# Moving a load, halving tile 0's modulation weights and reordering the first products of a decoder layer

## The chip, the cores and the metric

The kernel runs on one core of a Trainium2 chip. The metric is device time in microseconds (us) of one execution, a median over runs; lower is better. A core has TensorE (PE, matrix products into PSUM; its weight loads are PEld), VectorE (DVE), ScalarE (ACT) and GpSimd (POOL) for elementwise work, and SyncE (SP), which here only issues transfers. Each engine takes its instructions in program order and waits where one needs another engine's result or a transfer.

## The reference

One decoder layer on x (512 tokens by 1024 channels), conditioned by a vector c (1024), all in float32:

```python
cs = jax.nn.silu(c)
mod = cs @ w_ada[l] + b_ada[l]                       # 6 x 1024 numbers
shift1, scale1, gate1, shift2, scale2, gate2 = ...   # six pieces of mod
h = _rmsnorm(x, norm1_g[l]) * (1.0 + scale1) + shift1
proj = h @ w_in[l]                                   # queries, keys, values, gates
# sliding-window attention and differential attention on proj, gated merge, w_out,
# then a second modulated norm and a gated MLP with a causal convolution, final norm
```

The change concerns the first stage alone: shift1 and scale1, h, and the product of h with the first 768 columns of w_in.

## The kernel before, in words

The channels are cut into eight column tiles k = 0 to 7 of 128, the tokens into four row tiles. The first stage does, for every k: shift and scale of the tile's 128 channels (`mods[k]`), the normalised and modulated activations with channels on partitions (`hTh[k]`, 128 by 512), and their products with `w_in[128 k : 128 k + 128, 0:768]`, added into six PSUM banks `acc6` (six column groups, `FIRST` or `DONE` order). A float32 product is made of three passes on rounded operands: each operand is split into a high part (a cast, ScalarE) and a low part (the difference, VectorE), and the products high x high, low weight x high and high x low are added (`mm_k`: parts 0 and 2). `split_hi(k)` and `split_lo(k, part)` split the weights `w0[k]` into `w0h` and `w0l`; `h_tile(k)` writes `hTh[k]` and the unrounded `hf` on ScalarE, and `h_low(k)` their difference `hTl[k]` on VectorE. Tiles 6 and 7 of hT lie in a buffer called hThB, the others in hThA.

Shift and scale are sums over 1024 rows of w_ada. The weights of tile k (`adaw[k]`, 128 partitions by 2 by 8 by 128: j = 0 is scale, j = 1 shift, eight row groups kk) are multiplied by cs and added on VectorE and ScalarE (`ac_first`, `ac_ops`: `ac`), and a product with ones sums them over partitions (`reduce_mod`, into `pa`). For tile 0 TensorE multiplies five of the eight row groups directly with cs (`direct0`), VectorE adds up the other three (`add_a0`); for tile 1 TensorE does two of eight (`early_mod`, `direct`). `finish_mod(k)` makes `mods[k]` of `pa`, on VectorE and, for k > 0, one part on ScalarE. `h_turn(k)` (for tile 0, `turn`) transposes x on TensorE; x has been scaled by its reciprocal root mean square (`stat`, `root`, `scale_x`). `keep_warm` is TensorE filler whose result is not used.

What sets the order: in this stage SyncE issues all loads in one queue in the order of the code (`tc.manual_schedule` with SyncE): c, four tiles of x, then for each k the modulation weights and `w0[k]`, then small vectors, then the weights of later stages. TensorE, VectorE and ScalarE follow the code too. Work that the code writes further down, such as the casts of the next stage's weights (`split`, lines 127 to 129, the tiles `w_0_h` and so on, loaded in `load_cols`), is placed among the stage's instructions by a scheduler that works from estimated times, when the kernel is built.

## Time and profile before

| what | before |
|---|---|
| median of three runs | 685.49 us |
| lowest and highest run | 685.24, 686.26 us |
| span of the profiled execution, first to last instruction | 684.1 us |
| median of the runs less that span | 1.4 us |
| PE busy, and instructions | 675.3 us (99%), 4141 |
| DVE, ACT, POOL busy | 564.2, 384.5, 98.5 us |
| mean TensorE clock granted, of full speed | 0.998 |
| first product of the stage, last wait of PE | at 15.36 us, at 51.27 us |

The profiled execution's own time is its span, 684.1 us, and what lies around it before the first and after the last instruction; beside the median that is 1.4 us. In a row of the profile in order of time, the columns are the start in us from the first instruction, the duration in us, the engine, the line of the kernel, the operation, the tiles written and read, shapes and a count; in square brackets stands how long the engine had been idle and what ended that. SPq and ACTq are issues of transfers. In a row by stretches (A:B) the columns are the length, the busy time of PE, PEld, DVE, ACT and POOL with counts, then the granted clock of TensorE, the share of the transfer engines and GB/s; where only PE is shown, PE stands alone. In a row of waits: engine, tile and line that waited, for whom, total us, times, longest.

### The profile page before, as it was taken

Reading aid. Unit: us, or ns where it says so; the run is one execution under the profiler, and the core shown is the slowest. Engines: PE = TensorE matmul, PEld = TensorE weight load, DVE = VectorE, ACT = ScalarE, POOL = GpSimd, SP = SyncE. Lnnn points to the kernel's source line nnn. Section 1 sums busy time; section 2 is a strip of 40 time slices with the busy share of each in tenths; the row PEclk is TensorE's granted clock in tenths of the full one; section 3 lists DMA queues with packets and bytes.
Section 4 is the critical chain, followed back from the end, with each engine's and each line's share of the span. In section 5 each row is a group of like instructions: output and inputs, shape, how many; then the busy total and the mean of one; then the engine's idle time right before and its main releaser. Section 6 shows DMA issues by size and latency. Waiting matters only on the chain. (4 is left out here: it accounts for less than half of the span.)

```text
span 684.1 us, 11125 instructions
## 1 busy us (share of the span) xinstructions
PE 675.3 (99%) x4141; PEld 589.7 (86%) x4141; DVE 564.2 (82%) x1075; ACT 384.5 (56%) x688; POOL 98.5 (14%) x119
## 2 busy tenths in 40 slices
PE   9999999999999999999999999999999999999995
PEld 5887887878888888888899999999999998888885
DVE  4999875988796756974589988888888999979997
ACT  6776774546543223324377665666555665656765
POOL 3000000011012012021030111112120003440300
PEclk9999999999999999999999999999999999999999
DMA  9995422565456885659555788777978647995903
GB/s 304 349 296 181 144 62 64 163 166 162 144 157 181 255 246 158 217 144 345 187 93 109 170 216 212 180 165 207 216 194 216 153 170 186 191 205 146 166 1 123
DMA packets 117142, 123.89 MB, mean 181 GB/s; under 512 B 5063, under 2 KB 94184, under 8 KB 117088
## 3 DMA queue, kind: packets, MB, share of 16 engines
q1 hardware_dynamic: 97246, 95.11, 43.3%
q0 software_dynamic: 19648, 27.79, 24.1%
q8 instruction: 32, 0.52, 0.3%
q10 hardware_dynamic: 194, 0.28, 0.1%
q14 instruction: 22, 0.18, 0.1%
HBM read 118.97 MB, written 2.11 MB: 177 GB/s over the span
## 5 line engine op out<-in xcount | busy, mean ns | idle before, releaser
L1362 PE MATMUL up<-t,m_whi 128*128 128x256 f32 x512 | 93.1, 283 | 0.0
L1362 PEld LDWEIGHTS up<-t,m_whi 128*128 128x128 f32 x512 | 79.9, 192 | 0.0
L1362 PE MATMUL up<-t,m_wlo 128*128 128x256 f32 x256 | 72.4, 283 | 0.0
L1362 PE MATMUL up<-bh,p_whi 128*128 128x256 f32 x232 | 65.7, 283 | 0.0
L1362 PE MATMUL up<-bl,p_whi 128*128 128x256 f32 x232 | 65.7, 283 | 0.0
L1362 PE MATMUL up<-bh,p_wlo 128*128 128x256 f32 x232 | 65.7, 283 | 0.0
L952 POOL DMA_DIRECT2D arow<-arow x28 | 22.5, 804 | 247.8 <-DVE sd L821 123.6
L1362 PEld LDWEIGHTS up<-t,m_wlo 128*128 128x128 f32 x256 | 49.2, 192 | 0.0
L1271 POOL DMA_DIRECT2D s<-in_w_up_dram x21 | 26.9, 1353 | 141.3 <-DMA s<-in_w_up_dram 69.2
L1362 PEld LDWEIGHTS up<-bh,p_whi 128*128 128x128 f32 x232 | 44.5, 192 | 0.0
L1362 PEld LDWEIGHTS up<-bl,p_whi 128*128 128x128 f32 x232 | 44.5, 192 | 0.0
L1362 PEld LDWEIGHTS up<-bh,p_wlo 128*128 128x128 f32 x232 | 44.5, 192 | 0.0
L944 DVE SCALAR_TENSOR_TENSOR arow<-ra,cs,arow 128x512 f32<-128x512 f32 x56 | 41.8, 748 | 0.6
L1299 ACT CAST m_whi<-s 128x1024 fp32r<-128x1024 f32 x31 | 32.4, 1046 | 11.1 <-DVE s L1293 6.3
L1303 DVE TENSOR_TENSOR m_wlo<-s,m_whi 128x1024 fp32r<-128x1024 f32 x31 | 37.8, 1218 | 0.0
L1362 PE MATMUL up<-t,p_whi 128*128 128x256 f32 x176 | 32.2, 283 | 0.0
L1362 PEld LDWEIGHTS up<-t,p_whi 128*128 128x128 f32 x176 | 27.5, 192 | 0.0
L816 ACT ACTIVATE sd<-sd,dmx 128x128 f32<-128x128 f32 (+3 forms) x32 | 17.7, 557 | 17.3 <-DVE dmx L806 17.3
L1369 ACT ACTIVATE gT<-a,cv 128x512 f32<-128x512 f32 x22 | 17.7, 813 | 16.9 <-DVE a L1404 15.8
L1299 ACT CAST p_whi<-wa 128x1024 fp32r<-128x1024 f32 x18 | 18.7, 1041 | 12.6 <-PE up L1362 12.6
L1303 DVE TENSOR_TENSOR p_wlo<-wa,p_whi 128x1024 fp32r<-128x1024 f32 x18 | 22.0, 1222 | 3.8 <-ACT p_whi L1299 3.8
L1362 PE MATMUL up<-t,p_wlo 128*128 128x256 f32 x88 | 24.9, 283 | 0.0
(499 smaller groups left out, 2052.4 us busy)
## 6 DMA issues: line engine op xcount, KB each, us to landing
ra<-in_w_ada_dram SPq DMA_DIRECT2D x32, 512.0 KB, 4.9
wa<-in_w_up_dram SPq DMA_DIRECT2D x22, 512.0 KB, 4.2
s<-in_w_up_dram SPq DMA_DIRECT2D x21, 512.0 KB, 4.7
s<-in_w_up_dram POOLq DMA_DIRECT2D x21, 512.0 KB, 6.9
w<-in_w_in_dram SPq DMA_DIRECT2D x12, 512.0 KB, 5.0
a<-in_w_up_dram SPq DMA_DIRECT2D x11, 512.0 KB, 4.7
b<-in_w_down_dram SPq DMA_DIRECT2D x10, 512.0 KB, 4.2
adaw<-in_w_ada_dram SPq DMA_DIRECT2D x8, 512.0 KB, 6.3
```

Of the source, the lines that this page charges most:

```text
L816: exp = nc.scalar.activation(pm[m], pm[m], AF.Exp, bias=mx[:, m : m + 1], scale=slope, accum_out=ls)
L944: nc.vector.scalar_tensor_tensor(ac, r[:, a], cc, ac, ALU.mult, ALU.add)
L952: nc.gpsimd.dma_start(whole[0:n], whole[n : 2 * n], accum_op=ALU.add)
L1271: nc.gpsimd.dma_start(dst, upblock(*blk), accum_op=ALU.add)
L1299: nc.scalar.copy(W[J, name][0], R[J, SRC[name]])
L1303: nc.vector.tensor_sub(lo, R[J, SRC[name]], hi.bitcast(F32))
L1362: nc.tensor.matmul(o[u], w[:, k, cu], b[:, k], start=name in ("p1", "m5", "p2") and k == 0 and x == 0, stop=k == 3 and x == 2, skip_group_ ...
L1369: nc.scalar.activation(grow(j), av[J][:, u], AF.Identity, bias=cv[:, 66 + j : 67 + j], scale=cv[:, 44 + j : 45 + j])
```

## The change

- c is loaded from ScalarE's queue instead of SyncE's, where it was first.
- `adaw[0]` is loaded in four pieces instead of two: both halves of scale, then both of shift.
- VectorE no longer adds up any of tile 0's shift: TensorE multiplies all eight of its row groups, four before tile 3 of x is turned and four after.
- The filler of two products after tile 0's `finish_mod` is gone; `h_turn(1)` stands there.
- The first hT tile is written in two halves, one by VectorE and one by ScalarE.
- For k = 0 the products high x high of five groups come first, then those with the low weights.
- For tile 1 all direct products of scale and shift come early, the sixth group's products ahead of the sums, and `split_lo(1, 0)` after `finish_mod`.

```diff
@@ -163,7 +163,7 @@
 
 
     crow8 = cpool.tile([8, P], F32, name="crow8")
-    nc.sync.dma_start(crow8, c.rearrange("o (a p) -> (o a) p", p=P))
+    nc.scalar.dma_start(crow8, c.rearrange("o (a p) -> (o a) p", p=P))
     NR = 16 + 8 + 1
     rows = cpool.tile([NR, P], F32, name="rows")
     nc.scalar.dma_start(rows[0:16, :], b_ada[0, 0 : 2 * D].rearrange("(a p) -> a p", p=P))
@@ -226,9 +226,12 @@
             aw = big.tile([P, 2, KT, P], F32, tag="out" + "hl"[k // 3], name=f"adaw{k}")
         else:
             aw = pp.tile([P, 2, KT, P], F32, tag="adaw", bufs=2, name=f"adaw{k}")
-        cut = 4 if 0 < k < 5 else KT
-        for a in range(0, KT, cut):
-            for j, base in ((0, D), (1, 0)):
+        cut = 4 if k < 5 else KT
+        pieces = [(a, j) for a in range(0, KT, cut) for j in range(2)]
+        if k == 0:
+            pieces.sort(key=lambda e: e[1])
+        for a, j in pieces:
+            for base in ((D, 0)[j],):
                 nc.sync.dma_start(
                     aw[:, j, a : a + cut],
                     wada[a * P : (a + cut) * P, base + k * P : base + (k + 1) * P].rearrange("(a p) n -> p a n", p=P),
@@ -309,20 +312,20 @@
                 cs[:, kk : kk + 1].to_broadcast([P, P]),
                 start=start and kk == kks[0],
                 stop=stop and kk == kks[-1],
+                skip_group_check=True,
             )
 
     def early_mod(gi):
         pa = tbank(f"pa{gi}", (P, 2, P))
-        direct(pa, 0, gi, (6, 7))
+        for j in range(2):
+            direct(pa, j, gi, (6, 7), start=j == 0)
         return pa
 
     def reduce_mod(gi, early=None):
         pa = early or tbank(f"pa{gi}", (P, 2, P))
         for j in range(2):
             if early:
-                if j:
-                    direct(pa, 1, gi, (6, 7))
-                nc.tensor.matmul(pa[:, j], ac[gi][0][:, j], ones, start=False, stop=True)
+                nc.tensor.matmul(pa[:, j], ac[gi][0][:, j], ones, start=False, stop=True, skip_group_check=True)
             else:
                 nc.tensor.matmul(pa[:, j, 0:1], ac[gi][0][:, j], ones[:, 0:1], start=True, stop=True)
         return pa
@@ -380,7 +383,13 @@
     def h_tile(k, between=None):
         hf = pp.tile([P, S], F32, tag="hf", bufs=2, name=f"hf{k}")
         for dst in (hTh[k], hf):
-            nc.scalar.activation(dst, pts[k], AF.Identity, bias=mods[k][:, 1:2], scale=mods[k][:, 0:1])
+            sl = slice(0, S)
+            if k == 0 and dst is not hf:
+                nc.vector.tensor_scalar(
+                    dst[:, : S // 2], pts[k][:, : S // 2], mods[k][:, 0:1], mods[k][:, 1:2], ALU.mult, ALU.add
+                )
+                sl = slice(S // 2, S)
+            nc.scalar.activation(dst[:, sl], pts[k][:, sl], AF.Identity, bias=mods[k][:, 1:2], scale=mods[k][:, 0:1])
             if dst is not hf and between is not None:
                 between()
             if dst is not hf and k + 1 < ALONE:
@@ -397,12 +406,15 @@
         last = k == KT - 1
         if part == (2 if last else 1):
             return
-        for i in some:
-            for p in (1, 2) if last and part else (0, 1) if part == 0 and not last else (part,):
-                lhs, rhs = ((wh, hTh), (wl, hTh), (wh, hTl))[p]
-                nc.tensor.matmul(
-                    acc6[i], lhs[:, i * P : (i + 1) * P], rhs[k], start=k == 0 and p == 0, stop=last and p == 2
-                )
+        ps_ = (1, 2) if last and part else (0, 1) if part == 0 and not last else (part,)
+        order = [(i, p) for i in some for p in ps_]
+        if k == 0:
+            order.sort(key=lambda e: e[1])
+        for i, p in order:
+            lhs, rhs = ((wh, hTh), (wl, hTh), (wh, hTl))[p]
+            nc.tensor.matmul(
+                acc6[i], lhs[:, i * P : (i + 1) * P], rhs[k], start=k == 0 and p == 0, stop=last and p == 2
+            )
 
     keep_warm(WARM)
     rst = pp.tile([P, NT], F32, name="rst")
@@ -435,21 +447,22 @@
         nc.scalar.activation(xn[:, t, HEAD:], xn[:, t, HEAD:], AF.Copy, scale=rst[:, t : t + 1])
 
     pa0 = [tbank("pa0", (P, P)), acc6[4][:, :P]]
-    a0 = [pp.tile([P, P], F32, name=f"a0_{j}") for j in range(2)]
+    a0 = pp.tile([P, P], F32, name="a0")
     DIRECT = 5
 
-    def add_a0(j, kks):
+    def add_a0(kks):
         for kk in kks:
-            w, f = adaw[0][:, j, kk], cs[:, kk : kk + 1]
+            w, f = adaw[0][:, 0, kk], cs[:, kk : kk + 1]
             if kk == DIRECT:
-                nc.vector.tensor_scalar_mul(a0[j], w, f)
+                nc.vector.tensor_scalar_mul(a0, w, f)
             else:
-                nc.vector.scalar_tensor_tensor(a0[j], w, f, a0[j], ALU.mult, ALU.add)
-
-    def direct0(j):
-        for kk in range(DIRECT):
+                nc.vector.scalar_tensor_tensor(a0, w, f, a0, ALU.mult, ALU.add)
+
+    def direct0(j, kks, stop=False):
+        for kk in kks:
             nc.tensor.matmul(
-                pa0[j], adaw[0][:, j, kk], cs[:, kk : kk + 1].to_broadcast([P, P]), start=kk == 0, stop=False
+                pa0[j], adaw[0][:, j, kk], cs[:, kk : kk + 1].to_broadcast([P, P]), start=kk == 0,
+                stop=stop and kk == kks[-1],
             )
 
     for t in range(NT):
@@ -459,23 +472,22 @@
             turn(t - 1)
             keep_warm((4, 1)[t - 1])
     root(2)
-    add_a0(0, range(DIRECT, DIRECT + 2))
+    add_a0(range(DIRECT, DIRECT + 2))
     root(3)
-    add_a0(0, range(DIRECT + 2, KT))
-    add_a0(1, range(DIRECT, KT))
+    add_a0(range(DIRECT + 2, KT))
     scale_x(0)
     scale_head(2)
     scale_head(3)
     scale_x(1)
-    direct0(0)
+    direct0(0, range(DIRECT))
     turn(2)
-    direct0(1)
-    for j in range(2):
-        nc.tensor.matmul(pa0[j], a0[j], ones, start=False, stop=True)
+    direct0(1, range(4))
+    nc.tensor.matmul(pa0[0], a0, ones, start=False, stop=True)
     turn(3)
+    direct0(1, range(4, KT), True)
     finish_mod(0, pa0)
     split_hi(0, 0)
-    keep_warm(2)
+    h_turn(1)
     h_tile(0, lambda: split_hi(0, 1))
     split_lo(0, 0)
 
@@ -500,24 +512,21 @@
             nc.vector.tensor_scalar_mul(nsink, sink, -1.0)
             nc.vector.tensor_sub(nlam, ls[:, 1:2], ls[:, 0:1])
             nc.vector.tensor_scalar_add(nlam, nlam, -LAM_INIT)
-        if gi == 0:
-            h_turn(1)
         mm_k(gi, 0, DONE if gi else FIRST[:5])
         mm_k(gi, 1)
         if more:
+            early = None
             if gi == 0:
-                split_lo(1, 0)
-            pa = reduce_mod(gi + 1, early_mod(1) if gi == 0 else None)
-            if gi == 0:
+                early = early_mod(1)
                 mm_k(0, 0, FIRST[5:])
+            pa = reduce_mod(gi + 1, early)
             if ALONE <= gi + 2 < KT:
                 ac_first(gi + 2, 1)
                 ac_first(gi + 2, 0)
             if gi:
                 h_turn(gi + 1)
             last_mod = finish_mod(gi + 1, pa)
-            if gi:
-                split_lo(gi + 1, 0)
+            split_lo(gi + 1, 0)
             split_lo(gi + 1, 1)
             h_tile(gi + 1)
         mm_k(gi, 2)
```

The diff does not show where instructions outside these functions end up. The first place is ScalarE at the end of the stage. `mod_586`, `hThB<-xt_581` and `hf_591` are tile 6; `w0h_600` is tile 7's weights; `mod_632` and `xt_627` are tile 7; `w_0_704` and `w_0_710` are two weight loads of the next stage. Before:

```order
L288 ACTIVATE ac_0_579<-adaw_173,cs 128x256
L337 ACTIVATE mod_586<-pa_574,cols 128x1
L383 ACTIVATE hThB<-xt_581,mod_586 128x512
L383 ACTIVATE hf_591<-xt_581,mod_586 128x512
L361 CAST w0h_600<-w_7_176 128x512
L363 CAST w0h_600<-w_7_176 128x256
L128 CAST w_0_h<-w_0_704 128x1024
L128 CAST w_0_h<-w_0_710 128x1024
L337 ACTIVATE mod_632<-pa_624,cols 128x1
L383 ACTIVATE hThB<-xt_627,mod_632 128x512
L383 ACTIVATE hf_637<-xt_627,mod_632 128x512
L539 ACTIVATE qa<-a_110,qsc 128x512
```

With the change:

```order
L291 ACTIVATE ac_0_579<-adaw_175,cs 128x256
L128 CAST w_0_h<-w_0_704 128x1024
L340 ACTIVATE mod_586<-pa_574,cols 128x1
L392 ACTIVATE hThB<-xt_581,mod_586 128x512
L392 ACTIVATE hf_591<-xt_581,mod_586 128x512
L364 CAST w0h_600<-w_7_178 128x512
L366 CAST w0h_600<-w_7_178 128x256
L128 CAST w_0_h<-w_0_710 128x1024
L340 ACTIVATE mod_632<-pa_624,cols 128x1
L392 ACTIVATE hThB<-xt_627,mod_632 128x512
L392 ACTIVATE hf_637<-xt_627,mod_632 128x512
L548 ACTIVATE qa<-a_110,qsc 128x512
```

The cast of `w_0_704` has moved from behind tile 7's weight casts to ahead of tile 6's mod; the cast of `w_0_710` stands where it stood.

The second place is VectorE around the modulation of tile 1 (`mod_332` before, `mod_331` now), where `w0l_295` and `w0l_300` are the low weights of tile 1. Before:

```order
L300 SCALAR_TENSOR_TENSOR ac_0_289<-adaw_135,cs,ac_0_289 128x256
L301 TENSOR_TENSOR ac_0_289<-ac_0_289,ac_1_298 128x256
L391 TENSOR_TENSOR hTlA<-hf_286,hThA 128x512
L369 TENSOR_TENSOR w0l_295<-w_1_140,w0h_294 128x512
L333 SCALAR_TENSOR_TENSOR mod_332<-pa_323,cols 128x1
L371 TENSOR_TENSOR w0l_295<-w_1_140,w0h_294 128x256
L286 TENSOR_SCALAR ac_1_352<-adaw_142,cs 128x256
L300 SCALAR_TENSOR_TENSOR ac_1_352<-adaw_142,cs,ac_1_352 128x256 x2
```

With the change:

```order
L304 TENSOR_TENSOR ac_0_294<-ac_0_294,ac_1_303 128x256
L400 TENSOR_TENSOR hTlA<-hf_290,hThA 128x512
L336 SCALAR_TENSOR_TENSOR mod_331<-pa_322,cols 128x1
L372 TENSOR_TENSOR w0l_300<-w_1_142,w0h_299 128x512
L374 TENSOR_TENSOR w0l_300<-w_1_142,w0h_299 128x256
L289 TENSOR_SCALAR ac_1_352<-adaw_144,cs 128x256
L303 SCALAR_TENSOR_TENSOR ac_1_352<-adaw_144,cs,ac_1_352 128x256 x2
```

The 512-column subtraction has moved from ahead of mod to behind it.

The third place is TensorE from tile 0's modulation to the first product (`pa_206` and `pa_208` collect tile 0's scale, `a_111` its shift). Before:

```order
L451 MATMUL pa_206<-cs,adaw_130 128x128 x5
L432 MATMUL xt_205<-ident,xn 128x128
L451 MATMUL a_111<-cs,adaw_130 128x128 x5
L474 MATMUL pa_206<-ones,a_0_207 128x128
L474 MATMUL a_111<-ones,a_1_208 128x128
L432 MATMUL xt_205<-ident,xn 128x128
L184 MATMUL a_113<-ones 128x256
L378 MATMUL xt_307<-ident,xn 128x128 x4
L403 MATMUL a_110<-hThA,w0h_282 128x512
```

With the change:

```order
L463 MATMUL pa_208<-cs,adaw_130 128x128 x5
L444 MATMUL xt_207<-ident,xn 128x128
L463 MATMUL a_111<-cs,adaw_130 128x128 x4
L485 MATMUL pa_208<-ones,a_209 128x128
L444 MATMUL xt_207<-ident,xn 128x128
L463 MATMUL a_111<-cs,adaw_130 128x128 x4
L381 MATMUL xt_285<-ident,xn 128x128 x4
L415 MATMUL a_110<-hThA,w0h_282 128x512
```

The shift's direct products are eight instead of five, four of them behind the last turn of x; the sum over `a_1` and the filler are gone.

## The prediction

> **What bounds the kernel now.** I read the page first, then TensorE's waits, then the first 55 us in order of time, engine by engine.
>
> ```profile
> PE 675.3 (99%) x4141; PEld 589.7 (86%) x4141; DVE 564.2 (82%) x1075; ACT 384.5 (56%) x688; POOL 98.5 (14%) x119
> ...
> PE a L184 <- POOL ones L143: 1.0, 1, 1.0
> PE pc L262 <- POOL ident masks.py:199: 0.2, 1, 0.2
> PE a L403 <- ACT hThB L383: 0.2, 1, 0.2
> ```
>
> TensorE (PE) is the bound: busy for 99% of the span, and the list of all its waits is these three rows, 1.4 us together. So a delay that PE takes anywhere before its last product is paid to the end, and a gain counts only if PE's next work is ready sooner. The third row is the one that matters here. It stands at the end of the first stage, where a column tile's normalised activations (hThB) come late from ScalarE (ACT):
>
> ```profile
> 42.73 0.91 ACT L288 ACTIVATE ac<-adaw,cs 128x256 f32<-128x256 f32 x2 [0.61 <-DMA adaw<-in_w_ada_dram]
> 44.55 0.26 ACT L337 ACTIVATE mod<-pa,cols 128x1 f32<-128x1 f32 x1 [0.92 <-DVE mod L333]
> 44.86 0.78 ACT L383 ACTIVATE hThB<-xt,mod 128x512 fp32r<-128x512 f32 x1
> ...
> 47.58 1.05 ACT L128 CAST w_h<-w 128x1024 fp32r<-128x1024 f32 x1 [0.46 <-DMA w<-in_w_in_dram]
> 49.20 1.05 ACT L128 CAST w_h<-w 128x1024 fp32r<-128x1024 f32 x1 [0.57 <-DMA w<-in_w_in_dram]
> 50.15 0.25 ACT L337 ACTIVATE mod<-pa,cols 128x1 f32<-128x1 f32 x1
> 50.44 0.78 ACT L383 ACTIVATE hThB<-xt,mod 128x512 fp32r<-128x512 f32 x1
> ...
> 45.98 0.39 PE L403 MATMUL a<-hThB,w0h 128*128 128x512 f32 x1
> 46.21 0.39 PE L403 MATMUL a<-hThB,w0l 128*128 128x512 f32 x1
> ...
> 51.27 1.67 PE L403 MATMUL a<-hThB,w0h 128*128 128x512 f32 x6 [0.19 <-ACT hThB L383]
> ```
>
> The reader is to see two things. ACT does tile 6 (mod at 44.55, hThB at 44.86), and PE starts on it at 45.98. Only then does ACT come to two casts of weights for the next stage (w_h, line 128), and it sits idle before each until the weights have landed: at 47.58 and 49.20 data set the pace, not ACT. The second of these pushes tile 7's hThB to 50.44, and that is PE's only wait of the stage. ACT works in order, so whatever stands behind such a cast waits for the transfer too.
>
> **The change part by part.** I take the parts in the order of time, and the largest is last.
>
> c off SyncE's queue:
>
> ```profile
> 0.74 0.40 SPq L166 DMA_DIRECT2D crow<-in_c_dram  x1
> ...
> 1.20 1.78 SPq L245 DMA_DIRECT2D xn<-in_x_dram  x4
> ```
>
> One issue of 0.40 us leaves the queue and x is issued at 0.74 instead of 1.20: 0.46 earlier, and with it the stream behind it. ACT issues one transfer more, while it has nothing else to do than wait for x.
>
> Tile 0's modulation:
>
> ```profile
> 10.85 1.38 PE L451 MATMUL pa<-cs,adaw 128*128 128x128 f32 x10
> ...
> 12.41 1.38 PE L451 MATMUL a<-cs,adaw 128*128 128x128 f32 x10
> 13.63 0.39 PE L474 MATMUL pa<-ones,a 128*128 128x128 f32 x2
> 13.85 0.39 PE L474 MATMUL a<-ones,a 128*128 128x128 f32 x2
> ...
> 14.28 0.16 DVE L339 TENSOR_TENSOR mod<-a,cols 128x1 f32<-128x1 f32 x1
> 14.53 0.78 ACT L383 ACTIVATE hThA<-xt,mod 128x512 fp32r<-128x512 f32 x1 [0.59 <-DVE mod L339]
> 15.36 0.50 PE L403 MATMUL a<-hThA,w0h 128*128 128x512 f32 x1
> ```
>
> A product of this kind is two passes; 12.41 to 13.63 for ten is 0.12 a pass. Before, PE makes 12 products here (5, 5 and 2 that add VectorE's sums); now 14 (5, 4, 1, 4). PE can begin at about 10.4, when x tile 1 is turned and the first half of the weights is there (10.85 less 0.46). Then 10 passes (1.2), a turn (0.1), 8 (1.0), 2 (0.2), a turn (0.1) and 8 (1.0) end at 14.0. VectorE's last add began 0.43 after PE's last two passes had begun (13.85, 14.28), so now at about 13.8 + 0.43 = 14.2 instead of 14.28. The last half landed by 11.95 (12.41 less 0.46), so transfers no longer set this point: PE's own passes do. Gain 0.1.
>
> The first hT in halves on two engines: 0.78 for 512 columns; the 256-column activation of this page takes 0.49,
>
> ```profile
> 11.27 0.49 ACT L427 ACTIVATE xn<-xn,rst 128x256 f32<-128x256 f32 x1
> ```
>
> from another memory, so I take 0.55 and a gain of about 0.25. The first product moves from 15.36 to about 15.0; bounds 14.5 (the whole 0.46 and a half at half the price, 0.39) and 15.4 (nothing).
>
> High products first, tile 1's shift early, group 5 ahead of the sums, and split_lo(1, 0) moved behind finish_mod (VectorE's row order above). These go together:
>
> ```profile
> 18.34 0.69 DVE L369 TENSOR_TENSOR w0l<-w,w0h 128x512 fp32r<-128x512 f32 x1
> 19.30 0.22 DVE L333 SCALAR_TENSOR_TENSOR mod<-pa,cols 128x1 f32<-128x1 f32 x1 [0.28 <-PE pa L325]
> ...
> 22.90 0.42 DVE L301 TENSOR_TENSOR ac<-ac,ac 128x256 f32<-128x256 f32 x1
> ...
> PEld pa L327 <- DVE ac L301: 0.3, 1, 0.3
> ...
> 23.73 0.50 PE L327 MATMUL pa<-ones,ac 128*128 128x1 f32 x4
> ```
>
> The number of products is the same; two of them (0.23 each, as 46.21 follows 45.98) now stand ahead of the sums of tile 1. From 15.0: ten products 2.3, eight passes 0.9, two products 0.46, two sums 0.45: 19.1, so mod at about 19.2 against 19.30. VectorE (DVE) then still has the subtraction of 0.6 to 0.69 that it did from 18.34, before an idle time of 0.28. Its sum for tile 2 ended at 23.32, 4.02 after mod, with PE's weight load waiting 0.3 for it. Now 19.2 + 4.02 + 0.6 = 23.8: PE gets the sum 0.5 later and is late by about 0.4 (bounds -0.5, if PE still had all of its start, and +0.6). So the opening's gain is spent at tile 2, and PE, which has no idle time in the tiles after it, reaches tile 6 at 46.4 (45.5 to 46.6).
>
> **The moved cast.** The rows of ACT's order show the first cast of w_h now ahead of tile 6's mod and hThB; before, it stood behind them and behind tile 7's weights. What it waits for:
>
> ```profile
> 41.46 3.62 SPq L567 DMA_DIRECT2D w<-in_w_in_dram  x3
> ...
> DMA to landing us min/median/max: 6.1/6.2/7.0
> ...
> 20.00:24.00 4.00, 4.00 (x21) 3.28 (x20) 3.79 (x9) 4.00 (x8) 0.00 (x0) 1.00 1.13 364
> 42.00:44.00 2.00, 2.00 (x12) 1.65 (x11) 1.85 (x5) 1.03 (x3) 0.00 (x0) 1.00 0.55 171
> ```
>
> The weights are issued at 41.46 and land 6.1 us later, at 47.56; the cast starts at 47.58. The queue is full of earlier loads nearly all the way (364 GB/s), so the landing moves with the stream: 0.46 earlier, 47.12 (bounds 0 and 0.46, since no byte is removed). From the start of a cast to PE's first product behind it: 49.20 to 51.27, 2.07. So PE starts tile 6 at 47.12 + 2.07 = 49.19 instead of 45.98: 3.21 late. Tile 6 itself took 45.98 to 51.08 (51.27 less its wait of 0.19), 5.10, and in the new order nothing in it waits: tile 7's mod is wanted 1.43 ahead of PE's start on tile 7, as tile 6's was (44.55, 45.98), at 52.86. ACT comes to it earlier: from the start of hThB to the end of hf and tile 7's weight casts it took 2.26 (44.86 to 47.58 less the idle 0.46), and a cast takes 0.95 (49.20 to 50.15), so with hThB at 48.41 it is free at 51.6. PE starts tile 7 at 54.29. Against 51.27 that is **+3.02**. What came before is swallowed: PE would have been at tile 6 at 46.4 and waits 2.8 us (2.6 to 4.1); whatever the opening gains or loses only makes this wait longer or shorter, which is why the first parts do not enter the sum. Behind the cast in ACT's queue also stand hf and tile 7's weight casts; their products come after those of hThB.
>
> The profiled span is 684.1; the median of the runs is 685.49, 1.4 more, which lies around the span. The delay is added to both: 687.1 and 685.49 + 3.02 = **688.5**.
>
> **The rivals.**
>
> *No stall (the other side).* If w_h's weights landed by 44.0, the cast would be over when tile 6's mod is wanted (44.55 + 0.4), and only the opening would count: 685.49 + 0.4 = 685.9 (685.0 to 686.1). For it: the stream sags at 42 to 44, 2 us times (364 - 171)/364, about 1 us of transfer time that another rhythm of issues might give back. Against it: that and the 0.46 make 46.1, still 2 us late, and every microsecond short of 44.0 is paid in full. 8%.
>
> *The clock falls as well.* A wait of 2.8 us may be long enough for TensorE's clock to be halved. After the last product, at 676.9, the clock held for 4.9 us, to 681.8 (0.91 in the slice from 681 to 682 is a fall after 0.82 of it):
>
> ```profile
> 676.00:677.00 1.00, 0.93 (x8) 1.00 0.28 111
> 677.00:681.00 4.00, 0.00 (x0) 1.00 0.68 271
> 681.00:682.00 1.00, 0.00 (x0) 0.91 1.06 394
> ...
> 7.57 0.34 PEld L184 LDWEIGHTS a<-ones 128*128 128x128 f32 x1 [0.52 <-issue]
> ...
> 9.28 0.37 PEld L184 LDWEIGHTS a<-ones 128*128 128x128 f32 x2 [0.32 <-issue]
> ```
>
> At the start weight loads take 0.34 until 7.57 and 0.19 from 9.28, after 3 to 6 us of filler. If the clock fell, 3 to 6 us of half-speed work would cost 1.5 to 3 us more: 690.0 to 691.5, say 690.7. Against it: 2.8, and even 4.1, is under 4.9. 13%. [...]
>
> *Part is regained later.* PE's weight loads wait for ACT and DVE in the attention stage, at most 0.4 at a time:
>
> ```profile
> PEld td L835 <- DVE w_l L129: 0.4, 1, 0.4
> ```
>
> If two such waits hang on transfers, which now have 3 us more lead, 0.8 comes back: 687.7. Against it: the rows name computing engines, which move with PE. 9%.
>
> **How the numbers follow.** The forecast, a stall of about 3 us paid to the end, 70%: 688.5, own range 687.9 to 689.2 (the landing 0.46 later, PE up to 0.3 off). The range 687.2 to 690.3 adds the third rival and the lower end of the second, and leaves out no stall and a longer cold spell. A measurement of this kernel can tell about 0.2%, 1.37 us, from no change; the forecast and the last two rivals are all slower by more. No stall is nearly all within it. Slower 0.90, same 0.08, faster 0.02.
>
> **What would show it.** In the changed profile: ACT idle for 2 us or more before the first w_h cast near 47.1, with mod and hThB of tile 6 behind it; PE with one wait of 2.6 to 4.1 us on hThB near 49.2, and no wait before tile 7; the first product at 14.5 to 15.4; PE's sum of tile 2 at about 24.2; a granted clock of 1.00 through 45 to 60. It is wrong if the w_h cast starts before 45, if PE's wait on hThB is under 1 us, or if the time from PE's start on tile 6 to its last product is shorter than before.

## The result and the profile after

| what | before | after |
|---|---|---|
| median of the runs, same chip (5 each) | 686.04 us (685.24 to 687.56) | 688.54 us (688.09 to 688.90) |
| ratio, 95% interval | | 1.0036 (1.0023 to 1.0048) |
| profiled execution, span | 684.1 us | 686.3 us |
| mean TensorE clock granted | 0.998 | 0.998 |

The kernel became 2.5 us slower. Its median is the 688.5 that was forecast, but the rise that was forecast is 3.0: it was counted from 685.49, the median of three runs, and five runs of the kernel before give 686.04. And the trace shows another cause than the one that the forecast rested on. TensorE's (PE's) waits after the change, less two of 1.0 and 0.5 us for GpSimd's constants at the start:

```profile
PE pc L275 <- DMA rows<-in_diff_subln_g_dram: 1.7, 1, 1.7
PE a L415 <- ACT hThA L392: 1.1, 1, 1.1
...
PE pa L330 <- DVE ac L304: 0.3, 1, 0.3
```

There is no wait on hThB, neither at tile 6 nor at tile 7: the stall of 2.8 us that the prediction put at 49.19 us isn't there. Instead PE loses time at three places in the first 27 us. The same places in order of time (PE's matmuls, then two of VectorE's and three of ScalarE's instructions):

```profile
7.53 0.27 PE L275 MATMUL pc<-ident,rows 25*128 25x25 f32 x1 [1.73 <-DMA rows<-in_diff_subln_g_dram]
7.73 3.48 PE L184 MATMUL a<-ones 128*128 128x512 f32 x4
11.05 0.27 PE L444 MATMUL xt<-ident,xn 128*128 128x128 f32 x1
...
12.36 1.28 PE L463 MATMUL pa<-cs,adaw 128*128 128x128 f32 x10
...
17.35 0.50 PE L415 MATMUL a<-hThA,w0h 128*128 128x512 f32 x1 [1.05 <-ACT hThA L392]
...
26.52 0.58 PE L330 MATMUL pa<-ones,ac 128*128 128x1 f32 x4 [0.32 <-DVE ac L304]
...
48.73 0.39 PE L415 MATMUL a<-hThB,w0h 128*128 128x512 f32 x1
...
57.89 0.48 PE L132 MATMUL pq<-hThA,w_h 128*128 128x512 f32 x1
...
15.90 0.16 DVE L342 TENSOR_TENSOR mod<-a,cols 128x1 f32<-128x1 f32 x1 [0.78 <-PE a L463]
16.10 0.54 DVE L388 TENSOR_SCALAR hThA<-xt,mod 128x256 fp32r<-128x256 f32 x1
...
16.74 0.56 ACT L392 ACTIVATE hThA<-xt,mod 128x256 fp32r<-128x256 f32 x1 [2.75 <-DVE hThA L388]
...
46.03 1.05 ACT L128 CAST w_h<-w 128x1024 fp32r<-128x1024 f32 x1 [0.36 <-DMA w<-in_w_in_dram]
47.30 0.26 ACT L340 ACTIVATE mod<-pa,cols 128x1 f32<-128x1 f32 x1 [0.22 <-DVE mod L336]
```

Before, the turn of the same rows and the fillers behind it were these:

```profile
5.48 0.30 PE L272 MATMUL pc<-ident,rows 25*128 25x25 f32 x1
5.70 3.78 PE L184 MATMUL a<-ones 128*128 128x512 f32 x4
```

The reader is to see four things. First, the turn of `rows` (the bias row, the norm's gain, `diff_subln_g`), which ran at 5.48 us without a wait, now waits 1.7 us for their loads, and all that stands behind it on PE is late: the direct products of tile 0 start at 12.36 instead of 10.85. Second, the two halves of the first hT do not run beside each other: ScalarE's half starts only when VectorE's is done, and from VectorE's last add of the modulation to the first product it takes 17.35 - 15.90 = 1.45 us, where it took 15.36 - 14.28 = 1.08. Third, the sum of tile 2 waits 0.3 us for VectorE. Fourth, the moved cast of w_h (46.03) is over when tile 6's mod is wanted (47.30): ScalarE idles 0.22 us ahead of mod, and what it waits for there is VectorE.

The place where the next stage begins on PE is its first product into `pq`. Before:

```profile
55.59 0.48 PE L132 MATMUL pq<-hThA,w_h 128*128 128x512 f32 x1
```

From there to PE's last product it is 621.3 to 621.4 us in both (676.93 less 55.59, and 679.27 less 57.89). So what the first 58 us lose is paid to the end, as the prediction had it. I cut these 58 us into four stretches and use them for every kernel below, each from its own trace: the direct products' start, from there to the first product (hThA, w0h), from there to tile 6's first product, from there to `pq`. The medians stand beside them; kernels are named by what was done. The stretches are those of one execution of each kernel, the profiled one. Its time lies within 0.7 us of the kernel's median, but for "own products, mended", where it is 1.3 longer, so differences of a few tenths between stretches and medians mean nothing.

| kernel | direct starts | to first product | to tile 6 | to pq | pq at | median, us | ratio to before (95%) |
|---|---|---|---|---|---|---|---|
| before | 10.85 | 4.51 | 30.62 | 9.60 | 55.59 | 685.65 to 686.04 | 1 |
| the change | 12.36 | 4.99 | 31.38 | 9.15 | 57.89 | 688.54 | 1.0036 (1.0023, 1.0048) |
| cast held | 12.58 | 5.00 | 31.38 | 9.16 | 58.12 | 688.55 | 1.0041 (1.0029, 1.0054) |
| rows late | 10.17 | 5.11 | 33.03 | 9.29 | 57.60 | 687.77 | 1.0021 (1.0011, 1.0031) |
| rows late, cast held | 10.63 | 5.09 | 31.45 | 9.16 | 56.32 | 686.27 | 1.0007 (0.9998, 1.0016) |
| c back | 11.00 | 5.13 | 31.38 | 9.15 | 56.66 | 686.75 | 1.0012 (1.0003, 1.0020) |
| c only | 12.95 | 4.07 | 30.62 | 9.15 | 56.80 | 686.64 | 1.0009 (1.0001, 1.0018) |
| x held | 11.97 | 4.07 | 30.65 | 9.15 | 55.85 | 686.04 | 0.9998 (0.9989, 1.0007) |
| rows first | 14.98 | 4.07 | 30.63 | 9.15 | 58.83 | 688.90 | 1.0035 (1.0021, 1.0048) |
| halves apart | 11.00 | 4.43 | 31.34 | 9.15 | 55.92 | 685.94 | 0.9998 (0.9984, 1.0012) |
| lo early | 11.38 | 5.00 | 30.83 | 9.15 | 56.36 | 686.00 | 1.0003 (0.9995, 1.0012) |
| both, casts behind hf7 | 10.45 | 4.52 | 30.78 | 9.70 | 55.45 | 685.98 | 1.0005 (0.9997, 1.0014) |
| own products, mended | 10.64 | 4.26 | 31.04 | 9.15 | 55.09 | 685.53 | 0.9999 (0.9987, 1.0012) |
| the change, mended | 9.89 | 4.43 | 30.88 | 9.15 | 54.36 | 685.18 | 0.9992 (0.9983, 1.0000) |

For the change the four differences are +1.51, +0.48, +0.76 and -0.45: together +2.30 at `pq`.

### The profile page after: what moved, and what is told of

The parts are those of the page before. It is cut to its first block, busy times and chain, and to the rows that moved or that the text cites. A ratio compares the mean times of both kernels' runs of the same rounds, so it can differ in the third digit from the quotient of the medians.

```text
span 686.3 us, 11128 instructions
## 1 busy us (share of the span) xinstructions
PE 674.7 (98%) x4143; PEld 589.8 (86%) x4143; DVE 563.2 (82%) x1073; ACT 383.8 (56%) x688; POOL 98.3 (14%) x119
```

## The experiments

Each kernel ran beside the kernel before: 5 to 12 runs of the one, 25 to 35 of the other. Two theories stood against each other at first: that the moved cast makes the delay in some way that the waits hide (the prediction's cause), and that the late loads of `rows` make most of it, with the cast hidden beneath.

**Cast held.** The casts of the next stage's weights are issued only behind ScalarE's last weight cast of this stage, so ScalarE's order around tiles 6 and 7 is free of the moved cast.

```diff
-            nc.scalar.copy(wts[k][0][:, 512:768], w0[k][:, 512:768])
+            act_last[0] = nc.scalar.copy(wts[k][0][:, 512:768], w0[k][:, 512:768])
...
-    with tc.issue_after(last_mod.ins):
+    with tc.issue_after(last_mod.ins), tc.issue_after(act_last[0].ins):
         prefetch()
```

> The changed kernel with one difference: the cast of w_0_704 stands again behind tile 7's weight casts, as before the change. Theory 'cast' (the prediction's: the moved cast alone makes TensorE late at tile 6) expects TensorE on tile 6 at about 46.4 and the kernel within 0.4 of the kernel before. Theory 'rows' (the loads of bias and gain rows land behind x, TensorE waits 1.7 us for them near 7.5 and the whole stage is late; the cast hides under that) expects no gain over the change: first product at 17.3, tile 6 at 48.7, +2.5 (2.0 to 3.0) against the kernel before.

688.55 us, where the change has 688.54. The first w_h cast now starts at 49.99, and nothing is gained: from the first product to tile 6 it is 31.38 in both. In the change itself the moved cast costs nothing.

**Rows late.** The turn of `rows` and VectorE's four instructions on it stand behind the first turn of x; their results are first used in tile 0's modulation.

```diff
     keep_warm(WARM_EARLY)
-    nc.tensor.transpose(pc, rows, ident[:NR, :NR])
...
+    def turn_rows():
+        nc.tensor.transpose(pc, rows, ident[:NR, :NR])
...
             turn(t - 1)
+            if t == 1:
+                turn_rows()
             keep_warm((4, 1)[t - 1])
```

> The changed kernel with one difference: TensorE turns the bias and gain rows, and VectorE copies them, after the first tile of x has been turned instead of ahead of the last filler. The cast of w_0_704 stays ahead of tile 6. Theory 'rows' expects no wait of TensorE for rows, the first product at 15.2 to 15.8 instead of 17.35, and then the moved cast to show: it started at 46.0 after its transfer, and tile 6 follows 2.07 later, at 48.1, with TensorE waiting 1 to 2 us for it; so only 0.6 of the 2.5 comes back, +1.9 (1.4 to 2.5) against the kernel before. Theory 'cast' expects no gain at all, +2.5. A third, 'rows alone' (the moved cast is harmless even then), expects +0.4 or less.

687.77 us, 0.8 less than the change. The wait on the rows is gone and the first product is back at 15.28 us. Then the cast shows, in ScalarE's order of time and on PE:

```profile
46.24 1.05 ACT L128 CAST w_h<-w 128x1024 fp32r<-128x1024 f32 x1 [2.64 <-DMA w<-in_w_in_dram]
47.19 0.25 ACT L343 ACTIVATE mod<-pa,cols 128x1 f32<-128x1 f32 x1
47.48 0.78 ACT L395 ACTIVATE hThB<-xt,mod 128x512 fp32r<-128x512 f32 x1
...
48.31 0.50 PE L418 MATMUL a<-hThB,w0h 128*128 128x512 f32 x1 [1.49 <-ACT hThB L395]
```

This is the picture that was forecast for the change, ScalarE idle 2.64 us for the weights with mod behind them and PE waiting on hThB; it appears only when PE is early enough to notice. Not in every run, it seems: three of the nine took 686.6 to 686.7 us and the other six 687.6 to 688.1, and the trace is of one of the six. What the three did differently isn't on record.

**Rows late, cast held.** Both edits.

> Both differences at once: the rows turned after the first tile of x, and the cast of w_0_704 behind tile 7's weight casts. Theories 'rows' and 'cast' together expect what is left of the change without its two delays: first product at 15.2 to 15.8, the sum of tile 2 about 0.5 late by the subtraction that moved behind mod, and the time within +0.0 to +0.6 of the kernel before. If it is still 1 us or more slower, a third cause is at work.

686.27 us. The four corners, in medians: change 688.54, cast held 688.55, rows late 687.77, both 686.27. Holding the cast is worth 0.0 with the rows early and 1.5 with the rows late; mending the rows is worth 0.8 alone and 2.3 with the cast held. So two delays stand in parallel to a point: the late opening covers the cast wholly, and the cast covers part of the opening's. The median of this last kernel is 0.4 above the kernel before, which its interval doesn't tell from nothing; in its trace `pq` is 0.73 late, and the experiments on the halves and on `split_lo` below take that apart.

**c back, and c only.** In the change c goes back to SyncE's queue; in the kernel before c alone goes to ScalarE's.

```diff
-    nc.scalar.dma_start(crow8, c.rearrange("o (a p) -> (o a) p", p=P))
+    nc.sync.dma_start(crow8, c.rearrange("o (a p) -> (o a) p", p=P))
```

> The changed kernel with c loaded on SyncE's queue again, first, as before; all other edits kept. The scheduler then also puts the cast of w_0_704 back behind tile 7's weight casts. Theory 'rows' expects the rows to land before TensorE turns them at 5.5, no wait there, and the first product at 15.3 to 16.2 (x 0.46 later than in the change); the time +0.3 to +1.0 against the kernel before. Theory 'cast' expects +0.4 as well, so this run tells not between them but shows whether moving c back mends both delays.

> The kernel before with one edit of the change alone: c on ScalarE's queue. ScalarE's casts stay as before. If the move of c by itself makes the rows late (theory 'rows'), TensorE waits 1 to 1.7 us for them, the first product comes at 16.5 to 17.3 instead of 15.36, and the time is +1.0 to +1.9 against the kernel before. If the rows were late only through the other edits, it is -0.5 to +0.2.

686.75 and 686.64 us. With c back the rows are turned at 5.37 us without a wait. c alone, of all the edits, makes them wait, 1.1 us (its row, at 6.67, stands further down). At tile 6 the first is 1.53 us later than before, the second 1.66, and the whole change 2.75; at `pq` it is 1.07, 1.21 and 2.30. That the last sum comes out nearly even is chance, since each of the three has the same 0.45 taken off at tile 7 (explained below). The medians are 0.9, 1.0 and 2.5 above the kernel before. So c's move alone and the other edits alone cost about the same, and neither makes the whole loss. The rise of c only, 0.99, is at the lower end of what was expected (1.0 to 1.9). With c back the first w_h cast starts at 48.53, behind tile 6 again, with nothing done about its place, and with c alone moved it starts at 48.67; so it takes c's move and the other edits together to bring the cast forward. How the scheduler's estimates come to that was not followed.

**Why the rows are late: x held, and rows first.** Moving c does two things: x is issued 0.46 us earlier, and the rows go out behind c, 0.35 to 0.68 later. ScalarE's issues before the change, then after it:

```profile
0.74 0.40 ACTq L169 DMA_DIRECT2D rows<-in_b_ada_dram  x1
1.24 0.53 ACTq L170 DMA_DIRECT2D rows<-in_norm_g_dram  x1
1.79 0.23 ACTq L171 DMA_DIRECT2D rows<-in_diff_subln_g_dram  x1
```

```profile
0.74 0.58 ACTq L166 DMA_DIRECT2D crow<-in_c_dram  x1
1.42 0.33 ACTq L169 DMA_DIRECT2D rows<-in_b_ada_dram  x1
1.78 0.33 ACTq L170 DMA_DIRECT2D rows<-in_norm_g_dram  x1
2.14 0.28 ACTq L171 DMA_DIRECT2D rows<-in_diff_subln_g_dram  x1
```

The transfer queues' packets (q1 is SyncE's queue, q10 ScalarE's; packets, MB, share of the 16 engines' time), ScalarE's queue before the change from 0 to 2.5 us and from 2.5 to 8, then after it likewise, there with SyncE's queue from 2.5 to 8:

```profile
q10 hardware_dynamic: 46, 0.01, 2.0%
...
q10 hardware_dynamic: 4, 0.00, 0.3%
```

```profile
q10 hardware_dynamic: 14, 0.00, 0.6%
...
q1 hardware_dynamic: 564, 1.91, 97.5%
q10 hardware_dynamic: 52, 0.01, 1.1%
```

Before, 46 of the 50 small packets are through by 2.5 us; after, 14 of 66, and the other 52 go between 2.5 and 8 us, while x and w_ada keep the 16 engines 97.5% busy. Two kernels ask which of the two shifts it is. "x held" is c only, with a second load of c, into a tile that nobody reads, first on SyncE's queue, so that x goes out at 1.19 us again. "Rows first" is c only with c behind the three row loads.

```diff
+    spare8 = cpool.tile([8, P], F32, name="spare8")
+    nc.sync.dma_start(spare8, c.rearrange("o (a p) -> (o a) p", p=P))
```

> The kernel before, with c alone on ScalarE's queue, and a second load of c's 4 KB into a tile that nobody reads first on SyncE's queue, so that x is issued at about 1.20 us again, as before, while the rows' three loads still go out behind c (1.2 to 2.1 us). With c moved and nothing put in its place the rows' turn waited 1.1 us, the first product began at 17.02 and the run was 686.64. Theory 'x ahead': the rows came late because x's packets were queued ahead of theirs; with x back at 1.20 two of the rows' three loads are issued ahead of it or with it, and the wait goes to 0 to 0.6 us, first product 15.4 to 16.2, time 685.5 to 686.2. Theory 'issued later': it is the rows' own later issue that makes them late, whatever x does; the wait stays at 0.9 to 2 us, first product 16.6 to 17.4, time 686.3 to 687.0.

> The kernel before, with c on ScalarE's queue but behind the rows' three loads, which go out at 0.74, 1.24 and 1.79 us as before; x is alone on SyncE's queue, at 0.74. Theory 'issued later': the rows land as before (by 5.48), their turn waits for nothing, and what is late is c, issued last at about 2.1, whose turn at 2.85 us then waits 1 to 4 us and with it all that stands behind on TensorE: first product 15.4 to 18. Theory 'x ahead': the rows, now issued with x or behind it, wait 0.5 to 1.5 us all the same, and c too. If neither waits, the first product is at 14.9 to 15.4 by x's earlier issue, and the time 685.0 to 685.7.

```profile
PE pc L262 <- DMA crow<-in_c_dram: 4.4, 1, 4.4
```

With x held PE still waits 1.26 us for the rows (its row, at 6.79, stands below), so x's head start isn't needed for it: the rows' own later issue is enough. With the rows first (the row above) c, issued last at 2.07 us, comes at 7.0, about 5 us after its issue, where it took at most 2.1 before (issued 0.74, turned 2.85). The first product falls to 19.05, later than the 18 that I had allowed. The rows' turn shows no wait there, but that proves nothing: it stands behind c's on PE and ran at 9.6. ScalarE's queue tells more. It had moved 46 of its packets by 2.5 us before the change; with the rows first, issued at nearly the same times but with x at 0.74, it had moved none by then, 46 by 4.0 and 50, as many as the rows have, by 5.0; the first row load took 3.2 us to land instead of 1.6. So x's head start slows the rows as well, but alone it would not have held up a turn at 5.48. One load or the other is late: that small loads issued beside or behind x's can come microseconds later is shown; the law of the sharing is not. Before, the last row load went out at 1.79 us and was there by 5.48; with x held the second went out at 1.77 and the turn still stood until 6.79.

In the change ScalarE's queue moved no packet from 3.0 to 4.0 us, where SyncE's moved 110, and 30 from 4.0 to 5.0, beside SyncE's 96: a pause of at least 1 us. No run here separates one rule of sharing from another.

The time of x held, 686.04, is no slower than before although the wait stands, and its first product, at 16.04, is earlier than the 16.6 to 17.4 expected with such a wait; in both the expectation missed. Its stretches say why: direct products 1.12 late, of which 0.44 come back before the first product (the 4.07 of all three kernels in which c alone was moved, with w_ada landed by then) and 0.45 at tile 7 (below).

**A pause can cost more than itself while PE is still at half speed.** A filler of 512 columns takes 0.95 us at first (3.78 for four) and 0.50 later (1.98 for four). That is what half speed means here; the profile's granted clock reads 1.00 in both and doesn't show it. c only and x held have nearly the same wait, 1.14 and 1.26 us, but their direct products start 2.10 and 1.12 us later than before and their first products are 0.98 us apart. c only first, x held second, c back third:

```profile
6.67 0.27 PE L272 MATMUL pc<-ident,rows 25*128 25x25 f32 x1 [1.14 <-DMA rows<-in_norm_g_dram]
6.86 3.78 PE L184 MATMUL a<-ones 128*128 128x512 f32 x4
10.65 1.92 PE L184 MATMUL a<-ones 128*128 128x512 f32 x2
17.02 0.50 PE L403 MATMUL a<-hThA,w0h 128*128 128x512 f32 x1
```

```profile
6.79 0.27 PE L274 MATMUL pc<-ident,rows 25*128 25x25 f32 x1 [1.26 <-DMA rows<-in_norm_g_dram]
6.99 3.78 PE L186 MATMUL a<-ones 128*128 128x512 f32 x4
10.78 1.02 PE L186 MATMUL a<-ones 128*128 128x512 f32 x2
16.04 0.50 PE L405 MATMUL a<-hThA,w0h 128*128 128x512 f32 x1
```

```profile
5.54 1.98 PE L184 MATMUL a<-ones 128*128 128x512 f32 x4
9.38 0.33 PE L444 MATMUL xt<-ident,xn 128*128 128x128 f32 x1 [1.85 <-DVE xn L436]
```

The two fillers at 10.7 take 1.92 in one and 1.02 in the other: in c only PE was still at half speed. Fillers at half speed are real work on PE, and they pass the delay on. With c back PE was at full speed when the four fillers behind the rows began; they take 1.98 instead of 3.78, and PE then waits 1.85 us for x: there a delay of the rows of up to that length should have vanished in the gap, which no run tried.

**Halves apart.** Rows late and cast held, and x's row tiles 2 and 3 are turned into another PSUM bank, so that the two engines read their halves of tile 0 from two banks (`h_tile` is fitted to that, and writes hf in two pieces).

```diff
-        nc.tensor.transpose(pts[0][:, t * P : (t + 1) * P], xn[:, t, 0:P], ident)
+        to = pts[0] if t < 2 else acc6[5]
+        nc.tensor.transpose(to[:, t * P : (t + 1) * P], xn[:, t, 0:P], ident)
```

> The changed kernel with the rows turned late and the cast held (the pair that gave 1.0007) and one difference more: x tiles 2 and 3 of column tile 0 are turned into another PSUM bank, so that ScalarE's half of hT no longer waits for VectorE's half. If the halves in turn cost what the trace shows (1.45 us from VectorE's last add to the first product, 1.08 before the change), that stretch falls to 0.8 to 1.0 and the first product comes 0.4 to 0.6 earlier; the time falls by 0.2 to 0.5 against that pair, if VectorE's sum of tile 2 follows, and by nothing if the sum sets the pace.

```profile
14.54 0.16 DVE L346 TENSOR_TENSOR mod<-a,cols 128x1 f32<-128x1 f32 x1 [0.78 <-PE a L469]
14.74 0.54 DVE L395 TENSOR_SCALAR hThA<-xt,mod 128x256 fp32r<-128x256 f32 x1
...
14.74 0.56 ACT L397 ACTIVATE hThA<-a,mod 128x256 fp32r<-128x256 f32 x1 [0.86 <-DVE mod L346]
...
15.43 0.70 PE L420 MATMUL a<-hThA,w0h 128*128 128x512 f32 x2 [0.49 <-ACT hThA L397]
```

Both halves start at 14.74, and from the last add to the product it is 0.89 us: 0.19 less than before (1.08) and 0.56 less than in the change (1.45). So the halves work with two banks and are a loss of 0.37 with one. The first product comes 0.29 earlier, less than the 0.4 to 0.6 expected, since the direct products began 0.37 later in this execution. The median is 0.3 lower than without the edit, less than the intervals tell apart; the stretch shows it (5.09 to 4.43). In the change, where both halves are read from one bank, ScalarE's half is released by VectorE's and starts at 16.74, 0.64 us behind it; what imposes that order no run shows.

**Lo early.** Rows late and cast held, and `split_lo(1, 0)` ahead of the sums of tile 1.

```diff
                 early = early_mod(1)
+                split_lo(1, 0)
                 mm_k(0, 0, FIRST[5:])
...
-            split_lo(gi + 1, 0)
+            if gi:
+                split_lo(gi + 1, 0)
```

> The same pair with one difference: split_lo(1, 0) stands ahead of finish_mod of tile 1 again, as before the change. If that move costs what the prediction said (0.5 us at the sum of tile 2, where the pair shows a wait of 0.33), the wait is gone, tile 6 comes 0.3 to 0.5 earlier than 47.16 and the time falls by 0.3 to 0.5 against the pair.

PE's wait for VectorE's sum of tile 2 is gone, the sum comes 8.70 us after the first product instead of 9.19, and the stretch from first product to tile 6 is 30.83 instead of 31.45. 0.6 us is what the moved subtraction costs. Tile 6 itself comes at 47.21 and not, as expected, earlier than 47.16: the direct products began 0.75 later in this execution, at half speed for longer (its first eight fillers took 5.92 us, 4.07 without the edit). The median, 686.00 against 686.27, is too close to tell.

**All put right.** Three kernels join the mended parts. The first has rows late, two banks, split_lo early and the casts behind tile 7's hf; the second is the kernel before with its own products, c on ScalarE's queue, rows late, halves from two banks, two fillers less and the casts held; the third is the change with rows turned late and their three scalings later still, two banks, split_lo early and the casts held behind the last weight cast.

> The changed kernel with all mends at once: rows turned late, halves of hT in two banks, split_lo(1, 0) early, and both casts of the next stage's weights behind tile 7's hf. If the mends add up: first product near 15.2, no wait of TensorE at tile 2 or tile 7, tile 7 at 51.0 to 51.5 (51.27 before), and the time -0.6 to +0.1 against the kernel before. If it stays +0.4 or more, the change's own order of products costs something that these mends do not touch.

> The kernel before, with its own order of products and tile 0 in one piece, and of the change only c on ScalarE's queue and the first hT halved; the rows are turned behind x's second turn, the two halves of hT lie in two PSUM banks, two fillers ahead of the first product are left out, and the next stage's casts of the loaded weights are held behind ScalarE's last weight cast. If delay at the opening is paid one for one: first product 14.6 to 15.1, tile 7 at 50.6 to 51.0, next stage 54.9 to 55.3, time 684.5 to 685.4. If the sums of the later tiles set their own time, tile 7 stays at 51.3 and the time at 685.5 to 686.

> The change, with the rows turned behind x's second turn and their three scalings later still, the halves of hT in two PSUM banks, split_lo ahead of tile 2's modulation, and the next stage's casts held behind ScalarE's last weight cast. The same with the casts behind tile 7's hT had the first product at 14.97, tile 7 at 50.69, the next stage at 55.45 with a wait of 0.3 us for its first eviction, and 685.98. If the casts' place made that wait: next stage at 54.8 to 55.1, time 685.2 to 685.7. If not, 55.3 to 55.5 and 685.8 to 686.1.

685.98, 685.53 and 685.18 us. The first missed the range expected (at most 0.1 above the kernel before; it was 0.3): it lost at the next stage what it had won (9.70 in its last stretch, with a wait of 0.3 us for VectorE's first eviction, which stood behind the low parts of the cast weights). The second gained 0.5 us at `pq` and missed its range of 684.5 to 685.4 by little. In its profiled execution a weight split (`wbd`) came late at 298 us, with a wait of 0.9, and from `pq` to the end it took 622.8 instead of 621.3. That execution took 686.84, 1.3 more than the median, so it shows that half a microsecond won at the front need not arrive, not that it is usually lost. The third is ahead by 1.23 us at `pq`:

```profile
14.32 0.47 PE L422 MATMUL a<-hThA,w0h 128*128 128x512 f32 x1 [0.48 <-ACT hThA L399]
...
54.36 0.48 PE L132 MATMUL pq<-hThA,w_h 128*128 128x512 f32 x1
```

Its ratio is 0.9992 (0.9983 to 1.0000), some 0.6 us; the traced execution, at 684.57, was one of its two shortest. That is the best kernel of the study, and within what this measurement calls no change.

## Why the prediction was right in its number and wrong in its reason

**PE is the bound, and a delay is paid to the end.** Right: 621.3 to 621.4 us from `pq` to the end in every kernel but one.

**c off SyncE's queue, priced as a gain of up to 0.46.** This is the step that failed. The first tile of x did come 0.48 earlier, by ScalarE's first work on it, before and after:

```profile
4.73 1.06 ACT L414 ACTIVATE sq<-xn 128x1024 f32<-128x1024 f32 x1 [1.40 <-DMA xn<-in_x_dram]
...
4.25 1.06 ACT L426 ACTIVATE sq<-xn 128x1024 f32<-128x1024 f32 x1 [0.66 <-DMA xn<-in_x_dram]
```

But the step counted only what c no longer holds up, and not what it now stands ahead of on ScalarE's queue: the three small loads of `rows`, for whose turn PE waits, with four fillers and the first turn of x behind it. It put the first product at 15.0 with an upper bound of 15.4; it was 17.35. The turn of the rows began 2.05 later (1.73 of wait, 0.26 from c's turn, which waited for a constant of GpSimd's), and 0.54 of that came back by the direct products: +1.51. The 4.07 of the second stretch where c alone was moved is no gain of this step, since x held has it too, with x issued as late as before; the direct products there start so late that w_ada has landed.

**The halves, a gain of 0.25.** Wrong in sign: 0.37 lost, since both halves lie in one PSUM bank. Apart they gain 0.19, near the term. Each half took 0.54 to 0.56, as taken (0.55).

**High products first and split_lo behind mod.** Right: 31.4 us from the first product to tile 6 (15.0 to 46.4) was forecast, 31.38 measured, with the wait of 0.3 for tile 2's sum. That it starts 2.4 us later is the opening.

**The moved cast, +3.02 at tile 7.** The mechanism exists: with the opening mended, ScalarE waits for the weights with mod behind them, and from the start of the cast to PE's product it is 2.07 (46.24 to 48.31), as taken. But PE's wait was 1.5 us there and not 2.8, because the weights landed at 46.0 to 46.2 and not at 47.12, and PE was 0.4 later at tile 6 than the 46.4 assumed. In the change they were issued a microsecond earlier, at 40.43 instead of 41.46, so the landing moved by 1.5 (47.58 to 46.03 by the casts), three times what the stream was credited with. It isn't shown that the edits did that: rows late with and without the cast held, whose loads up to there are the same, issued these weights at 41.36 and 40.05, so a microsecond may be no more than what two executions differ by.

```profile
40.43 4.16 SPq L576 DMA_DIRECT2D w<-in_w_in_dram  x3
```

And in the change it is hidden: PE was late by 2.75 us already (48.73 against 45.98). The prediction said that what the opening gains or loses only makes this wait longer or shorter; it did not ask what happens if the opening loses more than the wait is long, where the wait is gone and the opening alone counts.

**Tile 7.** A gain that the sum lacked: before, PE's wait on tile 7's hThB, listed as 0.19 us, cost 0.45 in the last stretch (9.60 against 9.15 in nearly all other kernels). An opening that is late by that much loses nothing. The account of the change is +1.51 + 0.48 + 0.76 - 0.45 = +2.30 at `pq`; the profiled span rose by 2.2, the median by 2.5.

**The rivals.** The clock did not fall: it was granted in full from 44 to 54 us.

```profile
44.00:48.00 4.00, 4.00 (x23) 3.43 (x22) 3.55 (x9) 3.38 (x8) 0.00 (x0) 1.00 1.14 345
48.00:50.00 2.00, 2.00 (x10) 1.64 (x9) 2.00 (x6) 2.00 (x5) 0.00 (x0) 1.00 1.04 358
50.00:54.00 4.00, 4.00 (x24) 3.43 (x23) 3.60 (x8) 2.52 (x4) 0.00 (x0) 1.00 0.38 112
```

"No stall" came true as to the stall, but not by its condition (weights landed by 44.0; they came at 46.0) and not as to its time, since it kept the opening where it was. The cause that did it was in no rival: a wait that takes a removed one's place, at the loads beside the one that was moved. By the prediction's own tests the theory falls at two points, no wait on hThB and a shorter way from tile 6 to PE's last product (630.54 instead of 630.94 us). Two of its signs stayed away as well: the first product at 14.5 to 15.4 (17.35), and ScalarE idle for 2 us or more ahead of the first w_h cast (0.36). That the number held is luck: a loss of 2.3 that had not been foreseen took the place of one of 3.0 that had.

## What to carry to other kernels

When a load moves to another queue, list what stands behind it there, and which engine waits for those loads by name; a small load issued a microsecond later, behind a large transfer instead of ahead of it, can land 4 us later (c: by 2.85 when issued at 0.74, at 7.0 when issued at 2.07). Before a stall is added to a sum, ask from which delay further up it would vanish: two delays on one path that are not in series are worth the longer one, and mending one alone shows the other. Before an elementwise step is shared by two engines, look where its inputs lie: here the halves ran at the same time only with their inputs in two PSUM banks (both from 14.74 us), and one after the other from one (from 16.10 and 16.74).

## What the runs showed of the hardware that was not expected

Small loads behind a large one. c, 4 KB, came within 2.1 us of its issue as the first transfer, and about 5 us after it when issued at 2.07, behind three row loads on its own queue and three loads of x on the other (rows first).

PE came to full speed at very different times at the start, even between kernels whose fillers begin alike. At half speed a filler's weight load takes 0.34 us, later 0.15 to 0.19; the granted clock of the profile reads 1.00 in both. In the nine kernels without a pause at the rows the last single one of 0.34 begins between 4.05 and 7.57 us, with the same fillers from 3.0 to 3.4; in the five with a pause of 1.1 us or more ahead of the fillers, between 8.73 and 11.74. In the change it is at 9.60, and the two at 11.05 take 0.30 together:

```profile
9.60 0.34 PEld L184 LDWEIGHTS a<-ones 128*128 128x128 f32 x1 [0.52 <-issue]
11.05 0.30 PEld L184 LDWEIGHTS a<-ones 128*128 128x128 f32 x2 [0.37 <-issue]
```

Among kernels with the same start the moment so spreads over 3.5 us (4.05 to 7.57), and behind a pause it is later (8.73 to 11.74); that the pause is what delayed it wasn't tried by itself, and what sets the moment no run shows.
